# Down projection's weights and raws in the buffers of gate and up, and the last blocks' weights and features in slots that the last group does not read

## The chip, the core and the metric

One core of a Trainium2 chip runs the kernel. The metric is the device time of one execution in microseconds (us). The engines are TensorE (PE, with its weight loads as PEld), VectorE (DVE), ScalarE (ACT), GpSimd (POOL), and SyncE (SP), which issues most of the DMAs.

## What is computed

One layer of a hybrid decoder, for 1024 prompt tokens and 64 sample tokens (T = 1088 in all): a mixer (short gated convolution and a state-space scan between an input and an output projection), and behind it the feed-forward part to which the change belongs:

```python
D_MODEL = 1024
FFN_HIDDEN = -(-8 * D_MODEL // (3 * 256)) * 256      # 2816
...
    h2 = rmsnorm(x, g_ffn_pre) * (1 + scale_f) + shift_f
    f = (jax.nn.silu(h2 @ w_gate) * (h2 @ w_up)) @ w_down
    x = x + gate_f * rmsnorm(f, g_ffn_post)
```

All of it is in float32.

## The kernel before

A float32 operand is held as two parts, hi and lo, in a format that TensorE multiplies faster. `part(hi, lo, v)` makes them: ACT casts v to hi (L1039), DVE subtracts hi from v (L1040). A product is then three matmuls: hi by hi, hi by lo, lo by hi.

The hidden width 2816 is cut into 11 blocks j of 256. Gate, up and most of down use the Strassen-Winograd scheme: a `unit` makes the seven products p = 1, 5, 6, 3, 7, 2, 4 of one block of weights, in this order, each for the token halves q = 0 (PSUM banks `pm`, 256 columns) and q = 1 (banks `pz`, 288 columns). The first product into a result is copied out of PSUM by ACT (L1093), the others are added to it by DVE (L1095). ACT and DVE take their instructions in the order of the program, which a scheduler sets by its own costs; the products are held in the written order (`in_order`).

The features f = silu(gate) * up of each block are turned into hi and lo and stored to DRAM as f_d[j][q] (L1540), since they do not fit on the chip beside the weights. The last stretch of the program is:

- The last up unit, (10, [1]): block 10, half 1. Ahead of it, the raw weights of the first two down units (`raws_d`) are loaded into the pool `btp` of gate and up.
- Sixteen down units, here called u0 to u15: four groups of two blocks, g = [0,1], [2,3], [4,5], [6,7], by four pairs of row tiles mp = 0 to 3 of the output. `combos_d(g, mp)` makes a unit's seven weight combinations out of one raw tile: seven casts on ACT and seven subtractions on DVE, with four adds between them on POOL (L1652, L1654, L1655, L1658). The features of a group come back from DRAM into the slots `fc{j % 4}{q}`; those of the first group in three pieces each, the others whole, one slot at each of the units ahead (`ahead`). The results are gathered in `facc`.
- Blocks 8, 9 and 10 in plain form: `down(m)` does 18 matmuls for each of the eight row tiles m, for token tiles ts = [0,1,2,3] (block 1, 512 columns), then [4,5,6], then [7,8]. Their weights are `wd` (six tiles of 128 rows, split by `part` out of `rwd`), their features `ff`, both loaded on SP's queue: `rwd` first, then `ff` in the order of `queued_behind`, then the gate and the residual rows.
- The tail of each block (L1239 to L1256), which transposes, norms, adds the residual and stores.

Before, the down stage had pools of its own: `raw2` with five raw tiles and `wc2` with fifteen tiles of one product each. The last stage's pools were opened over them: `wdp` lay partly over `wc2`, `ff80` and `ff90` over `raw2`, and the two `rwd` buffers over slots of `fc1`. A tile in such a place waits for what used the place before.

Of the kernel before, what the change touches and what calls it, by code (L numbers as in the profile page):

```python
# [9 lines left out]
F32 = mybir.dt.float32  # L10
F32R = mybir.dt.float32r
# [5 lines left out]
P = 128  # L17
D = 1024
# [15 lines left out]
def hymba_step(ctx, tc, i, o):  # L34
    nc = tc.nc
# [992 lines left out]
    def in_turn(pools):  # L1028
        pools.append(pools.pop(0))
        return pools[-1]  # L1030
# [358 lines left out]

    left.close()  # L1390
    mid.close()
    slots = pool(left, "wcA", 4), pool(left, "wcB", 4)
    raw_from = [slots[0]] * 4
    xc0 = pool(left, "xc0", 1)
    sg0, f0, st0 = (pool(left, n, 1) for n in ("sg0", "f0", "st0"))
# [203 lines left out]
    w_from += [pool(right, "wcC", 2, side="right")] * 2  # L1599
    groups = [0, 1], [2, 3], [4, 5], [6, 7]  # L1600

    def raw_d(p, g, mp, tag="raw"):
        raw = p.tile([P, 4, 256], F32, tag=tag, name=nm("raw"))
        nc.sync.dma_start(raw, w_down[g[0] * 256:(g[-1] + 1) * 256, mp * 256:mp * 256 + 256].rearrange(
            "(k p) n -> p k n", p=P))
        return raw

    for j, qs in [(1, [1])] + [(j, [0, 1]) for j in range(2, 10)] + [(10, [0]), (10, [1])]:
        eng = nc.gpsimd if len(qs) == 2 else nc.vector
        gate_unit(j, qs, combos_w(w_gate, 256 * j, eng))  # L1610
        W = combos_w(w_up, 256 * j, eng)
        if (j, qs) == (10, [1]):

            raws_d = [raw_d(btp, groups[0], mp, "bt") for mp in range(2)]
        up_unit(j, qs, W, {}, eng)


    for stage in (left, base, right):
        stage.close()
    facc_of = [pool(right, f"facc{mp}", 1, side="right").tile([P, 2, T], F32, tag="facc", name=f"facc{mp}")  # L1620
               for mp in (3, 2, 1, 0)][::-1]
    facc = [facc_of[m // 2][:, m % 2] for m in range(KT)]
    raw2 = pool(left, "raw2", 5)
    wc2 = pool(left, "wc2", 15)
    fcp = [[pool(left, f"fc{n}{q}", 1) for q in range(2)] for n in range(4)]

    f_in, loads = {}, []
# [7 lines left out]
        f_in[j, q] = {p: [F[:, (at + s * nb + b) * n:(at + s * nb + b + 1) * n] for s in range(2)]  # L1635
                      for p, (at, nb, b) in AT.items()}

    def combos_d(g, mp):
        nk = len(g)
        raw = raws_d.pop(0) if raws_d else raw_d(raw2, g, mp)  # L1640
        A = raw.rearrange("p (k j) (i c) -> p i j k c", j=2, i=2)
        a11, a12, a21, a22 = (A[:, m, j] for m in range(2) for j in range(2))
        W = {}

        def parts_(p, b):
            t = wc2.tile([P, 2, 2, P], F32R, tag="wc2", name=nm(f"w{p}_"))[:, :, :nk]
            part(t[:, 0], t[:, 1], b)
            W[p] = [[t[:, s, k] for k in range(nk)] for s in range(2)]

        parts_(1, a11)  # L1650
        parts_(4, a22)
        nc.gpsimd.tensor_tensor(a22, a21, a22, op=add)  # L1652
        parts_(5, a22)
        nc.gpsimd.tensor_tensor(a21, a11, a21, op=sub)  # L1654
        nc.gpsimd.tensor_tensor(a11, a22, a11, op=sub)  # L1655
        parts_(6, a11)
        parts_(2, a12)
        nc.gpsimd.tensor_tensor(a12, a12, a11, op=sub)  # L1658
        parts_(3, a12)
        parts_(7, a21)  # L1660
        return W
# [7 lines left out]
    for g, nxt in itertools.zip_longest(groups, groups[1:], fillvalue=()):  # L1669
        ahead = [(j, q) for q in range(2) for j in nxt]  # L1670
        F = [{p: [[f_in[j, q][p][s] for j in g] for s in range(2)] for p in AT} for q in range(2)]
        for mp in range(4):
            W = combos_d(g, mp)

            for jq in ahead[mp:mp + 1]:
                load_f(*jq)
                nc.sync.dma_start(*loads[-1])
            out = [facc_of[mp][:, :, t0:t0 + 2 * n].rearrange("p m (h c) -> p m h c", h=2) for t0, n in QS]
            unit(W, F, len(g), [0, 1], lambda q, i, h: out[q][:, i, h], g == groups[0])


    left.close()
    ffp, rows_of = {}, []
    for at in ((8, 0), (9, 0), None, (8, 1), None, (10, 0)):
        if at:
            ffp[at] = pool(left, f"ff{at[0]}{at[1]}", 1)
        else:
            rows_of.append(pool(left, f"row{len(rows_of)}", 1))
    wdp, rwd = pool(left, "wdp", 6), pool(left, "rwd", 2)
    ffp.update({(j, 1): pool(left, f"ff{j}1", 1) for j in (9, 10)})  # L1690
    rowp, gfp, sqp = pool(left, "rowp", 11), pool(left, "gfp", 2), pool(left, "sqp", 1)

    wide = rows_of[1]
    rows_of = [rowp] * 11 + rows_of

    def row_end():
        p = in_turn(rows_of)
        return p.tile([P, 1280 if p is wide else D], F32, tag="row", name=nm("row"))[:, :D]

    def out_tail(ts):  # L1700
        res = []
# [17 lines left out]
                             ((0, 4), (4, 2), (6, 2)), (), (slice(0, 512), slice(512, D)), squares)  # L1719

    wd = []
    for k in range(6):
        v = wdp.tile([P, 2, D], F32R, tag="wd", name=nm("wd"))
        raw = rwd.tile([P, D], F32, tag="rwd", name=nm("rwd"))
        nc.sync.dma_start(raw, w_down[(16 + k) * P:(17 + k) * P, :])
        part(v[:, 0], v[:, 1], raw)
        wd.append((v[:, 0], v[:, 1]))
    ff = {}
    for q, (t0, n) in enumerate(QS):
        for j in (8, 9, 10):  # L1730
# [56 lines left out]
```

## Time and profile before

| | us |
|---|---|
| runs: lowest, median, highest of three | 1760.15, 1762.36, 1763.54 |
| profiled execution, its own time | 1754.62 |
| its span in the trace | 1752.9 |
| last up unit's end, u0's start | 1461.2 |
| u15's last add in facc | 1639.06 |
| first matmul of block 1 | 1654.96 |
| share of the span: PE, DVE, ACT, POOL | 96%, 65%, 44%, 11% |

The profiled execution is one of its own and lies 7.7 us below the median of the timed runs; sums over its rows are made against its own time. The mean granted clock of TensorE in it is 0.987 of full speed.

In rows of a timeline stand the start, the duration, the engine, the line in the kernel, the operation, out<-in, and in brackets the idle time ahead of it with what ended it; ACTq and SPq are those engines' DMA issues. In a row of windows stand, for each engine, its busy time and the number of instructions, then the granted clock of TensorE, the DMA engines' share and GB/s. A clock under 1.00 means that TensorE ran a part of that stretch at a lower speed.

### The profile page before, as it was taken

The numbers are of one execution on the slowest core, as the hardware profiler recorded it, in microseconds if no ns is written. First come the engines' busy times: TensorE is split into PE (matmuls) and PEld (weight loads), VectorE is DVE, ScalarE is ACT, GpSimd is POOL, SyncE is SP. The second block draws the span as 40 slices with busy tenths as digits, with TensorE's granted clock in tenths as the row PEclk, the third lists the DMA queues.
The fourth block names the chain that finished last, engine by engine and source line by source line (L and its number), as shares of the span: only waits on it lengthen the run. The fifth ranks groups of instructions, "written<-read, shape, count | busy, mean of one in ns | idle before, by whom it ended". The sixth has DMA issues, their size and how long they took to land.

```text
span 1752.9 us, 31332 instructions
## 1 busy us (share of the span) xinstructions
PE 1684.0 (96%) x12604; PEld 1598.2 (91%) x12604; DVE 1140.6 (65%) x2178; ACT 771.8 (44%) x1571; POOL 196.5 (11%) x293
## 2 busy tenths in 40 slices
PE   5999999999999999999999999999999999999697
PEld 4898888898999999998889999999999999999587
DVE  5588777777888686641147789566755584687434
ACT  3457454557444333322227665444544453422122
POOL 2110000000001000000000000222222002322012
PEclk9999999999999999999999999999999999999899
DMA  9210345442402421276365544334443259750433
GB/s 319 71 32 18 127 136 170 129 125 76 151 25 100 151 100 54 100 269 226 119 202 188 190 147 166 112 138 150 155 148 126 100 187 378 289 227 26 163 125 136
DMA packets 159671, 256.37 MB, mean 146 GB/s; under 512 B 10625, under 2 KB 123441, under 8 KB 157990
## 3 DMA queue, kind: packets, MB, share of 16 engines
q1 hardware_dynamic: 159238, 253.19, 41.9%
q8 instruction: 99, 1.62, 0.4%
q10 hardware_dynamic: 288, 1.18, 0.2%
q14 instruction: 46, 0.38, 0.1%
HBM read 184.63 MB, written 69.71 MB: 145 GB/s over the span
## 4 chain that ended last, share of the span: by engine, by line
PE 84%; DVE 6%; DMA 4%; ACT 3%; issue 2%; POOL 1%; SPq 1%; ACTq 0%; DVEq 0%; POOLq 0%
PE pm L334 10%; PE pm L336 10%; PE pm L335 10%; PE pz L1078 7%; PE pz L1080 7%; PE pz L1079 7%; PE pm L1078 7%; PE pm L1080 7%; PE pm L1079 7%; DMA h<-in_w_ada 1%; PE pm L209 1%; PE pz L751 1%; PE pz L745 1%; PE pz L756 1%; DMA raw<-in_w_in 1%
## 5 line engine op out<-in xcount | busy, mean ns | idle before, releaser
L312 DVE TENSOR_TENSOR wl<-raw,wh 128x512 fp32r<-128x512 f32 (+1 forms) x87 | 61.3, 729 | 99.6 <-ACT wh L311 85.8
L334 PE MATMUL pm<-h,wh 128*128 128x384 f32 (+1 forms) x342 | 114.3, 334 | 0.0
L335 PE MATMUL pm<-h,wh 128*128 128x384 f32 (+1 forms) x342 | 114.2, 334 | 0.0
L336 PE MATMUL pm<-h,wl 128*128 128x384 f32 (+1 forms) x342 | 113.5, 333 | 0.0
L336 PE MATMUL pm<-hb,wl 128*128 128x512 f32 (+2 forms) x320 | 107.3, 337 | 2.1 <-DVE wl L312 2.1
L335 PE MATMUL pm<-hb,wh 128*128 128x512 f32 (+2 forms) x320 | 107.5, 337 | 0.0
L311 ACT CAST wh<-raw 128x512 fp32r<-128x512 f32 (+1 forms) x89 | 56.4, 664 | 115.5 <-PE pm L335 72.7
L334 PE MATMUL pm<-hb,wh 128*128 128x512 f32 (+2 forms) x320 | 105.7, 337 | 1.0 <-ACT wh L311 1.0
L1040 DVE TENSOR_TENSOR fs<-f,fs 128x576 fp32r<-128x576 f32 (+2 forms) x76 | 53.5, 718 | 23.6 <-ACT fs L1039 22.8
L336 PEld LDWEIGHTS pm<-hb,wl 128*128 128x128 f32 x320 | 60.8, 190 | 7.6 <-DVE wl L312 2.4
L334 PEld LDWEIGHTS pm<-hb,wh 128*128 128x128 f32 x320 | 60.4, 190 | 6.8 <-ACT wh L311 1.2
L334 PEld LDWEIGHTS pm<-h,wh 128*128 128x128 f32 x342 | 64.8, 189 | 1.8 <-issue 0.9
L335 PEld LDWEIGHTS pm<-h,wh 128*128 128x128 f32 x342 | 64.7, 189 | 1.4 <-issue 0.7
L336 PEld LDWEIGHTS pm<-h,wl 128*128 128x128 f32 x342 | 64.7, 189 | 1.3 <-issue 1.0
L334 PE MATMUL pm<-ff,wd 128*128 128x512 f32 (+2 forms) x144 | 49.5, 344 | 16.8 <-DMA ff<-f_d 16.7
L335 PEld LDWEIGHTS pm<-hb,wh 128*128 128x128 f32 x320 | 60.7, 190 | 5.2
L1039 ACT CAST fs<-f 128x576 fp32r<-128x576 f32 (+2 forms) x76 | 44.5, 600 | 40.1 <-DMA f_d<-fs 25.0
L1095 DVE TENSOR_TENSOR facc<-facc,pz 128x288 f32<-128x288 f32 x96 | 43.3, 451 | 17.1 <-PE pz L1080 16.6
L334 PE MATMUL pm<-bt,wh 128*128 128x384 f32 (+2 forms) x146 | 50.9, 348 | 0.0
L1749 DVE TENSOR_TENSOR facc<-facc,pm 128x512 f32<-128x512 f32 (+2 forms) x24 | 12.7, 531 | 55.4 <-PE pm L336 55.4
L336 PE MATMUL pm<-ff,wd 128*128 128x512 f32 (+2 forms) x144 | 48.6, 338 | 0.0
L335 PE MATMUL pm<-ff,wd 128*128 128x512 f32 (+2 forms) x144 | 48.6, 338 | 0.0
(7118 smaller groups left out, 6331.4 us busy)
## 6 DMA issues: line engine op xcount, KB each, us to landing
raw<-in_w_in SPq DMA_DIRECT2D x48, 512.0 KB
wa<-in_w_ada SPq DMA_DIRECT2D x32, 512.0 KB
raw<-in_w_out SPq DMA_DIRECT2D x32, 512.0 KB
f_d<-fs SPq DMA_DIRECT2D x28, 576.0 KB
f_d<-fs SPq DMA_DIRECT2D x30, 512.0 KB
raw<-in_w_gate SPq DMA_DIRECT2D x28, 512.0 KB
raw<-in_w_up SPq DMA_DIRECT2D x28, 512.0 KB
y_d<-y SPq DMA_DIRECT2D x26, 544.0 KB
```

Of the source, the lines that this page charges most:

```text
L209: mm(ps[32 * j:32 * j + 32, :], cT[:, k, :], w[:, jj * 512:(jj + 1) * 512], start=(k == 0), stop=(k == KT - 1))
L311: (nc.gpsimd.tensor_copy if hi_eng else nc.scalar.copy)(wh, raw)
L312: (eng or nc.vector).tensor_tensor(wl, raw, wh, op=sub)
L334: mm(ps[:, :n], wh, xh, start=(first and j == 0), stop=False)
L335: mm(ps[:, :n], wh, xl, start=False, stop=False)
L336: mm(ps[:, :n], wl, xh, start=False, stop=(last and j == end))
L1039: nc.scalar.copy(hi, v)
L1040: (eng or nc.vector).tensor_tensor(lo, v, hi, op=sub)
L1078: mm(ps, W[0][k], X[0][k], start=(start and k == 0), stop=False, skip_group_check=True)
L1079: mm(ps, W[0][k], X[1][k], start=False, stop=False, skip_group_check=True)
L1080: mm(ps, W[1][k], X[0][k], start=False, stop=(stop and k == nk - 1), skip_group_check=True)
L1095: nc.vector.tensor_tensor(out(q, i, h), out(q, i, h), ps, op=add)
```

## The change

It has three parts.

1. The down units' raws go into `btp` (four tiles), and their weight combinations into `wcA` and `wcB` of gate and up, two products to one tile in the order of their use: 1 and 5, 6 and 3, 7 and 2, 4. A unit takes four of the eight tiles. `raw2` and `wc2` go, and `btp`, `wcA` and `wcB` are closed at the end of the down units only.
2. The four adds of `combos_d` are on DVE for group [0,1], and on POOL as before for the others.
3. The last stage is laid out anew. `wdp` and `ff90` lie over the slots of blocks 4 and 5, which the group [6,7] does not read. `ff80` and `ff100` lie over `btp`, and the halves 1 of the features over `wcA`, `wcB` and feature slots. The raw buffer of `wd` is the place of `ff90`: three loads of 256 rows use it one after the other instead of six of 128 rows through two buffers. There are 13 row tiles as before.

```diff
     left.close()
     mid.close()
-    slots = pool(left, "wcA", 4), pool(left, "wcB", 4)
+    kept_pools = ExitStack()
+    slots = pool(kept_pools, "wcA", 4), pool(kept_pools, "wcB", 4)
...
-    def raw_d(p, g, mp, tag="raw"):
-        raw = p.tile([P, 4, 256], F32, tag=tag, name=nm("raw"))
+    def raw_d(g, mp):
+        raw = btp.tile([P, 4, 256], F32, tag="bt", name=nm("raw"))
...
-    for stage in (left, base, right):
-        stage.close()
+    left.close()
+    right.close()
...
-    raw2 = pool(left, "raw2", 5)
-    wc2 = pool(left, "wc2", 15)
     fcp = [[pool(left, f"fc{n}{q}", 1) for q in range(2)] for n in range(4)]
...
-    def combos_d(g, mp):
+    w_from = [slots[0]] * 4 + [slots[1]] * 4
+
+    def combos_d(g, mp, eng):
         nk = len(g)
-        raw = raws_d.pop(0) if raws_d else raw_d(raw2, g, mp)
+        raw = raws_d.pop(0) if raws_d else raw_d(g, mp)
...
+        pair = [in_turn(w_from).tile([P, 2, 2, 2, P], F32R, tag="wc", name=nm("wd")) for _ in range(4)]
+
         def parts_(p, b):
-            t = wc2.tile([P, 2, 2, P], F32R, tag="wc2", name=nm(f"w{p}_"))[:, :, :nk]
+            n = (1, 5, 6, 3, 7, 2, 4).index(p)
+            t = pair[n // 2][:, n % 2]
             part(t[:, 0], t[:, 1], b)
...
-        nc.gpsimd.tensor_tensor(a22, a21, a22, op=add)
+        eng.tensor_tensor(a22, a21, a22, op=add)
         parts_(5, a22)
-        nc.gpsimd.tensor_tensor(a21, a11, a21, op=sub)
-        nc.gpsimd.tensor_tensor(a11, a22, a11, op=sub)
+        eng.tensor_tensor(a21, a11, a21, op=sub)
+        eng.tensor_tensor(a11, a22, a11, op=sub)
...
-        nc.gpsimd.tensor_tensor(a12, a12, a11, op=sub)
+        eng.tensor_tensor(a12, a12, a11, op=sub)
...
-            W = combos_d(g, mp)
+            W = combos_d(g, mp, nc.vector if g == groups[0] else nc.gpsimd)
...
-    left.close()
-    ffp, rows_of = {}, []
-    for at in ((8, 0), (9, 0), None, (8, 1), None, (10, 0)):
...
-    wdp, rwd = pool(left, "wdp", 6), pool(left, "rwd", 2)
-    ffp.update({(j, 1): pool(left, f"ff{j}1", 1) for j in (9, 10)})
-    rowp, gfp, sqp = pool(left, "rowp", 11), pool(left, "gfp", 2), pool(left, "sqp", 1)
+    for stage in (left, kept_pools, base):
+        stage.close()
...
+    ff_pools((8, 0), (10, 0), (8, 1))
+    rowa = pool(left, "rowa", 2)
+    ff_pools((9, 1))
+    rowb = pool(left, "rowb", 2)
+    wdp = pool(left, "wdp", 6)
+    ff_pools((9, 0), (10, 1))
+    rowp, gfp, sqp = pool(left, "rowp", 9), pool(left, "gfp", 2), pool(left, "sqp", 1)
+    rows_of = [rowa] * 2 + [rowb] * 2 + [rowp] * 9
...
-    for k in range(6):
-        v = wdp.tile([P, 2, D], F32R, tag="wd", name=nm("wd"))
-        raw = rwd.tile([P, D], F32, tag="rwd", name=nm("rwd"))
-        nc.sync.dma_start(raw, w_down[(16 + k) * P:(17 + k) * P, :])
-        part(v[:, 0], v[:, 1], raw)
-        wd.append((v[:, 0], v[:, 1]))
+    for k in range(0, 6, 2):
+        raw = ffp[9, 0].tile([P, 2, D], F32, tag="ff", name=nm("rwd"))
+        nc.sync.dma_start(raw, w_down[(16 + k) * P:(18 + k) * P, :].rearrange("(k p) n -> p k n", p=P))
+        for kk in range(2):
+            v = wdp.tile([P, 2, D], F32R, tag="wd", name=nm("wd"))
+            part(v[:, 0], v[:, 1], raw[:, kk])
+            wd.append((v[:, 0], v[:, 1]))
```

The order of the instructions moves at three places. In the names of both kernels raw_1668 and raw_1669 are the raws of u0 and u1; w1 to w7 are combinations, w3__1666 and w7__1667 those of the last up unit. In the names of after, a combination's tile is wd_ as well (wd_1680 to wd_1683 for u0, wd_1691 to wd_1694 for u1), and wd_1867 to wd_1874 are the six tiles of blocks 8 to 10.

On DVE, from the last up unit to u0. Before:

```order
L1095 TENSOR_TENSOR f_1670_15643<-f_1670_15643,pz_1672_15658 128x288
L1095 TENSOR_TENSOR f_1670_15643<-f_1670_15643,pz_1671_15644 128x288
L1095 TENSOR_TENSOR f_1670_15643<-f_1670_15643,pz_1673_15711 128x288
L1040 TENSOR_TENSOR w1__1680_15822<-raw_1668_15639,w1__1680_15822 128x256
L1040 TENSOR_TENSOR w4__1681_15825<-raw_1668_15639,w4__1681_15825 128x256
L1040 TENSOR_TENSOR w5__1682_15829<-raw_1668_15639,w5__1682_15829 128x256
L1525 TENSOR_TENSOR f_1670_15643<-f_1670_15643,sg_1655_15514 128x1152
```

After, the same stretch begins inside the last up unit's own combinations:

```order
L1040 TENSOR_TENSOR w3__1666_15633<-raw_1660_15612,w3__1666_15633 128x512
L1657 TENSOR_TENSOR raw_1668_15639<-raw_1668_15639 128x2x128
L1659 TENSOR_TENSOR raw_1668_15639<-raw_1668_15639 128x2x128
L1040 TENSOR_TENSOR wd_1680_15813<-raw_1668_15639,wd_1680_15813 128x256
L1660 TENSOR_TENSOR raw_1668_15639<-raw_1668_15639 128x2x128
L1040 TENSOR_TENSOR w7__1667_15636<-raw_1659_15610,w7__1667_15636 128x512
L1040 TENSOR_TENSOR wd_1681_15814<-raw_1668_15639,wd_1681_15814 128x256
L1040 TENSOR_TENSOR wd_1682_15815<-raw_1668_15639,wd_1682_15815 128x256 x2
L1663 TENSOR_TENSOR raw_1668_15639<-raw_1668_15639 128x2x128
L1040 TENSOR_TENSOR wd_1681_15814<-raw_1668_15639,wd_1681_15814 128x256
L1040 TENSOR_TENSOR wd_1691_15941<-raw_1669_15641,wd_1691_15941 128x256
L1095 TENSOR_TENSOR f_1670_15643<-f_1670_15643,pz_1672_15658 128x288
```

All of u0's combinations, with their four adds, now stand on DVE ahead of the last three adds into f; before, they stood behind them.

On ACT, at the last two units. Before, the casts into wd follow all the casts of u15:

```order
L1039 CAST w2__1905_17824<-raw_1900_17807 128x256
L1039 CAST w3__1906_17828<-raw_1900_17807 128x256
L1039 CAST w7__1907_17831<-raw_1900_17807 128x256
L1039 CAST wd_1914_17987<-rwd_1915_17988 128x1024
L1039 CAST wd_1916_17992<-rwd_1917_17993 128x1024
L1039 CAST wd_1918_17997<-rwd_1919_17998 128x1024
```

After (raw_1844 and raw_1855 are the raws of u14 and u15):

```order
L1039 CAST wd_1846_17628<-raw_1844_17625 128x256
L1039 CAST wd_1870_17938<-rwd_1869_17936 128x1024
L1039 CAST wd_1871_17941<-rwd_1869_17936 128x1024
L1039 CAST wd_1859_17758<-raw_1855_17753 128x256
L1039 CAST wd_1856_17755<-raw_1855_17753 128x256
L1039 CAST wd_1857_17756<-raw_1855_17753 128x256
L1039 CAST wd_1858_17757<-raw_1855_17753 128x256 x2
L1039 CAST wd_1857_17756<-raw_1855_17753 128x256
L1039 CAST wd_1873_17946<-rwd_1872_17944 128x1024
L1039 CAST wd_1874_17949<-rwd_1872_17944 128x1024
```

The casts of the second load now stand ahead of u15's; those of the first (wd_1867, wd_1868) stand further up among u14's, and those of the third behind u15's.

On SP, the loads behind the last raws. Before:

```order
L1604 DMA raw_1900_17807<-in_w_down 128x4x256
L1725 DMA rwd_1915_17988<-in_w_down 128x1024
L1725 DMA rwd_1917_17993<-in_w_down 128x1024
L1725 DMA rwd_1919_17998<-in_w_down 128x1024
L1725 DMA rwd_1921_18003<-in_w_down 128x1024
L1725 DMA rwd_1923_18008<-in_w_down 128x1024
L1725 DMA rwd_1925_18013<-in_w_down 128x1024
L1445 DMA ff_1926_18017<-f_d8_0_140 128x1024 x2
```

After:

```order
L1605 DMA raw_1855_17753<-in_w_down 128x4x256
L1732 DMA rwd_1866_17928<-in_w_down 128x2x1024
L1732 DMA rwd_1869_17936<-in_w_down 128x2x1024
L1732 DMA rwd_1872_17944<-in_w_down 128x2x1024
L1446 DMA ff_1875_17952<-f_d8_0_140 128x1024 x2
L1446 DMA ff_1876_17955<-f_d9_0_142 128x1024 x2
L1446 DMA ff_1877_17958<-f_d10_0_144 128x1024 x2
```

Three loads of 1 MB stand where six of 0.5 MB stood, ahead of the same feature loads.

More of the change, by code (lines that the diff above doesn't have):

```diff
@@ L1612, in hymba_step @@
         if (j, qs) == (10, [1]):
-            raws_d = [raw_d(btp, groups[0], mp, "bt") for mp in range(2)]
+            raws_d = [raw_d(groups[0], mp) for mp in range(2)]
         up_unit(j, qs, W, {}, eng)
-    for stage in (left, base, right):
-        stage.close()
+    left.close()
+    right.close()
     facc_of = [pool(right, f"facc{mp}", 1, side="right").tile([P, 2, T], F32, tag="facc", name=f"facc{mp}")
@@ L1679, in hymba_step, with ff_pools @@
             unit(W, F, len(g), [0, 1], lambda q, i, h: out[q][:, i, h], g == groups[0])
-    left.close()
-    ffp, rows_of = {}, []
-    for at in ((8, 0), (9, 0), None, (8, 1), None, (10, 0)):
[L1685 to L1688, printed above, removed]
-    wdp, rwd = pool(left, "wdp", 6), pool(left, "rwd", 2)
-    ffp.update({(j, 1): pool(left, f"ff{j}1", 1) for j in (9, 10)})
-    rowp, gfp, sqp = pool(left, "rowp", 11), pool(left, "gfp", 2), pool(left, "sqp", 1)
-    wide = rows_of[1]
-    rows_of = [rowp] * 11 + rows_of
+    for stage in (left, kept_pools, base):
+        stage.close()
+    ffp = {}
+    def ff_pools(*at):
+        for j, q in at:
+            ffp[j, q] = pool(left, f"ff{j}{q}", 1)
+    ff_pools((8, 0), (10, 0), (8, 1))
[6 more added lines that the diff above has]
+    rows_of = [rowa] * 2 + [rowb] * 2 + [rowp] * 9
     def row_end():
-        p = in_turn(rows_of)
-        return p.tile([P, 1280 if p is wide else D], F32, tag="row", name=nm("row"))[:, :D]
+        return in_turn(rows_of).tile([P, D], F32, tag="row", name=nm("row"))
     def out_tail(ts):
```

## The prediction

> **What bounds the kernel now.** First the page of the profile: its span, TensorE's share, and TensorE (PE) and its granted clock over 40 slices of 43.8 us.
>
> ```profile
> span 1752.9 us, 31332 instructions
> PE 1684.0 (96%) x12604; PEld 1598.2 (91%) x12604; DVE 1140.6 (65%) x2178; ACT 771.8 (44%) x1571; POOL 196.5 (11%) x293
> PE   5999999999999999999999999999999999999697
> PEclk9999999999999999999999999999999999999899
> ```
>
> TensorE is the bound, so only its gaps and its slow clock can be won. Between the first and the last slice only the 38th is weak (1621 to 1665 us): the last down units and the first block behind them. TensorE's waits for the lines of the down projection (line, releaser: us, times, longest):
>
> ```profile
> PE pm L334 <- DMA ff<-f_d: 16.7, 3, 15.9
> PE pm L1078 <- ACT facc L1093: 3.2, 2, 2.8
> PE pm L1078 <- DVE facc L1095: 1.8, 2, 1.4
> ```
>
> Then windows cut at the unit starts: the last up unit, u0 to u5, u13, u15, the gap, the rest of the first row of block 1 (one of its eight row tiles m), and the seven rows after it.
>
> ```profile
> core 0: us, PE busy (x) PEld busy (x) DVE busy (x) ACT busy (x) POOL busy (x), PEclk, DMA share, GB/s
> 1450.70:1461.20 10.50, 10.50 (x82) 10.50 (x81) 2.73 (x6) 3.33 (x7) 0.13 (x1) 1.00 1.02 414
> 1461.20:1476.90 15.70, 12.75 (x87) 12.02 (x85) 10.16 (x19) 6.86 (x19) 6.04 (x8) 0.89 0.88 342
> 1476.90:1487.43 10.53, 10.53 (x86) 10.53 (x85) 4.50 (x11) 4.42 (x13) 2.68 (x4) 1.00 1.05 417
> 1487.43:1498.87 11.44, 11.07 (x87) 10.60 (x85) 5.57 (x14) 5.96 (x19) 3.76 (x6) 1.00 0.93 333
> 1498.87:1510.13 11.26, 10.85 (x86) 10.60 (x85) 6.46 (x18) 6.26 (x19) 4.18 (x6) 1.00 0.29 91
> 1510.13:1523.00 12.87, 11.30 (x87) 10.66 (x85) 9.18 (x25) 4.45 (x13) 4.86 (x7) 1.00 1.00 400
> 1523.00:1533.48 10.48, 10.48 (x86) 10.48 (x85) 8.88 (x23) 2.85 (x7) 3.01 (x4) 1.00 0.92 359
> 1607.00:1617.48 10.48, 10.48 (x86) 10.48 (x85) 8.38 (x22) 2.85 (x7) 3.08 (x5) 1.00 0.01 2
> 1628.60:1639.10 10.50, 10.43 (x84) 10.19 (x82) 6.09 (x15) 0.04 (x1) 0.00 (x0) 1.00 0.01 2
> 1639.10:1654.90 15.80, 0.00 (x0) 0.00 (x0) 7.22 (x7) 6.13 (x6) 0.00 (x0) 0.62 0.59 186
> 1654.90:1663.10 8.20, 7.29 (x19) 4.53 (x20) 0.46 (x1) 0.00 (x0) 0.00 (x0) 0.68 1.02 403
> 1663.10:1691.70 28.60, 28.60 (x128) 23.63 (x127) 4.82 (x8) 0.00 (x0) 0.00 (x0) 1.00 0.53 190
> ```
>
> An undisturbed unit is 10.48 us (u5, u13). Over that, u0 loses 5.22, u1 0.05, u2 0.96, u3 0.78, u4 2.39: 9.40 us at the transition. At the other end TensorE stands still for 15.8 us and then runs at clock 0.68. The timelines of that place:
>
> ```profile
> 1639.06 1.99 ACT L1039 CAST wd<-rwd 128x1024 fp32r<-128x1024 f32 x2 [22.16 <-PE pz L1080]
> 1654.13 1.23 DVE L1040 TENSOR_TENSOR wd<-rwd,wd 128x1024 fp32r<-128x1024 f32 x1 [1.51 <-ACT wd L1039]
> 1596.92 52.60 SPq L1725 DMA_DIRECT2D rwd<-in_w_down  x6
> 1649.63 10.15 SPq L1445 DMA_DIRECT2D ff<-f_d  x12
> 1639.06 0.46 DVE L1095 TENSOR_TENSOR facc<-facc,pz 128x288 f32<-128x288 f32 x1 [0.37 <-PE pz L1080]
> 1663.11 0.69 DVE L1749 TENSOR_TENSOR facc<-facc,pm 128x512 f32<-128x512 f32 x1 [7.75 <-PE pm L336]
> ```
>
> The first cast into wd waits for the last product (1639.06). Its raw buffers come free one by one, so SP is held in its six rwd loads for 52.6 us, and the ff loads behind them start only at 1649.63. The wait is booked to ff, but it begins with where wd lies.
>
> **The change, part by part.** *Term A, the last group into block 1.* The order shows the wd casts and subtractions between the combinations of u13 to u15, and the ff loads behind three rwd loads. Block 1's first row can then end one period after the last unit: a row is 28.60/7 = 4.09 us (last window); the last unit's last add stands at 1639.06, the add of row 0 at 1663.11, and 24.05 - 4.09 = 19.96 us go. That includes the slow clock: matmuls start 0.42 apart in the first 5 us, some eleven of them, later 0.23.
>
> ```profile
> 1655.53 0.63 PE L335 MATMUL pm<-ff,wd 128*128 128x512 f32 x1
> 1655.95 0.63 PE L336 MATMUL pm<-ff,wd 128*128 128x512 f32 x1
> 1663.14 0.39 PE L335 MATMUL pm<-ff,wd 128*128 128x512 f32 x1
> 1663.37 0.39 PE L336 MATMUL pm<-ff,wd 128*128 128x512 f32 x1
> ```
>
> Does everything land in time? In before, the first rwd load goes at u12's start (1596.92), when u11 has left its slot; so it will now. Throughput over 1595 to 1665 us, in slices of 1.75 us:
>
> ```profile
> GB/s 0 105 363 131 9 0 0 0 0 0 0 0 9 0 0 0 0 0 0 0 0 0 9 0 0 0 0 295 225 80 236 192 318 250 344 414 421 418 413 411
> ```
>
> 1 MB goes through slices 2 to 4, so it has landed 4.6 us after its issue, as estimated from this row. One buffer serves three loads, and a load waits for both splits of the one before. A load and its two splits (1.04 and 1.23 each, the casts ahead of the subtractions) are some 8.1 us bare; between the unit's own rows I put them at one unit, 10.5: the third is split at u14 + 10.4 us. Then ff90, by the same row, lands at u14 + 15.0, and ff100, 1 MB at 411 GB/s or 2.5 us on, at u14 + 17.5; u15 ends at u14 + 20.96. Slack 3.5 us. ff80 goes into raw buffers that are free earlier. The loads of the other half and the gate and residual rows then start earlier than before, with block 1 (8 × 4.09 = 32.7 us) as cover; without it each 1 MB would cost 2.5 us.
>
> *Term B, the transition.* Before, u0's combinations go from DVE to POOL to ACT to DVE in turn, and start only when the last up unit drains.
>
> ```profile
> 1469.48 0.58 PE L1078 MATMUL pm<-fc,w__1685_15841 128*128 128x256 f32 x1 [2.84 <-ACT facc L1093]
> 1466.84 0.41 ACT L1039 CAST w__1685_15841<-raw 128x256 fp32r<-128x256 f32 x1 [0.85 <-POOL raw L1658]
> 1466.90 1.81 ACTq L1540 DMA_DIRECT2D f_d<-fs  x2
> 1465.53 1.28 POOL L1658 TENSOR_TENSOR raw<-raw 128x256 f32<-128x256 f32 x1 [2.03 <-DVE w__1684_15837 L1040]
> 1460.18 0.42 DVE L1040 TENSOR_TENSOR w__1680_15822<-raw,w__1680_15822 128x256 fp32r<-128x256 f32 x1
> 1462.28 0.63 DVE L1040 TENSOR_TENSOR w__1682_15829<-raw,w__1682_15829 128x256 fp32r<-128x256 f32 x1 [1.34 <-ACT w__1682_15829 L1039]
> ```
>
> ACT's copies out of PSUM, which release the bank, queue behind a cast that waits for POOL, and behind two stores. In the order of after, u0's and u1's combinations stand among those of the last up unit, 7 to 10 us earlier, and group 0's adds are on DVE. An add of that shape costs DVE about the 0.42 of the subtraction, 1.7 a unit, where u1 to u3 leave it 4.8 to 6 us free (windows). What stays: in u0 the third feature pieces and the two stores on ACT (1.81 us), estimated 1.0 us; in u3 and u4, where group 1 uses POOL as before and DVE is at 9.18 of 12.87, 0.9. So 9.4 - 1.9 = 7.5 us go. Bounds: 0 (the copies stay late for the stores' sake) and 9.4. I take 7.5, since only 1.81 of the chain stays on ACT. Two units' 14 subtractions and 8 adds are 9.2 us of DVE, into a stretch that has 7.8 free and, for u1's part, u0 behind it. Six of them stand ahead of the last up unit's w3 and w7 (2.5 us); if PE waits for these I allow 1 us, in the upper end alone.
>
> *Term C, the wd splits move beside units.* DVE gets six subtractions, ACT six casts:
>
> ```profile
> L1039 ACT CAST wd<-rwd x6: 1039/1044/1045, 1639.1 to 1653.1; 128x1024 fp32r<-128x1024 f32 x6
> L1040 DVE TENSOR_TENSOR wd<-rwd,wd x6: 1218/1226/1226, 1640.1 to 1654.1; 128x1024 fp32r<-128x1024 f32 x6
> ```
>
> ACT (2.85 of 10.48 busy) hides 2.1 a unit. DVE has 10.48 - 8.38 = 2.1 free in u13 and gets 2 × 1.23 = 2.45: a lag of 0.35 a unit, 1.05 after three, which u15 with 4.4 us free works off. A bank is used again one product pair (10.48/7 = 1.50 us) after it is full, and the add that reads it takes 0.46: PE bears 1.04 us of lag, but a single 1.23 ahead of an add can exceed it. I take +0.5. Bounds: 0, and 6 × 1.23 - 3 × 1.6 (u5's free time) = 2.6, plus 1.3 if each subtraction meets a POOL add and stretches as the 0.63 above does against 0.42: +3.9.
>
> The longest of POOL's four adds, 0.80 us in the mean (group by form):
>
> ```profile
> L1655 POOL TENSOR_TENSOR raw<-raw 128x256 f32<-128x256 f32 x16 | 12.8, 800 | 1.3
> ```
>
> Here a rule speaks against the change: the Trainium skill, "SBUF — State Buffer", section "SBUF: two separate sides", has a VectorE operation with two SBUF inputs and a GpSimd operation exclude each other for the whole instruction. The 0.63 row next to a POOL add agrees in kind. By the rule six subtractions could each lose a POOL add's 0.80, 4.8 us of DVE (estimate), and the sum would be a gain of 22 or 23 instead of 27. I keep the row's 0.21 each, in the upper bound alone, since POOL is busy 3.08 of 10.48 in u13.
>
> The rest (smaller pool count, 293 to 277 POOL rows, closing of pools) costs TensorE nothing: POOL is 11% busy. The pairing of two products in one tile frees weights up to 1.5 us later; u5 and u13 show PE without a wait, with the combinations of a unit needed a unit later.
>
> **Sum.** -20.0 - 7.5 + 0.5 = -27.0 us: the profiled execution 1754.6 becomes 1727.6. That execution lies 7.7 us below the median of the three runs, 1762.36; I predict the median, 1735.4.
>
> **Rivals.** R1: only block 1 gains; u0 to u4 lose their 9.4 again, because the copies wait behind stores and the features' loads (342 and 417 GB/s in u0 and u1, near the most any window shows). -19.5: 1742.9. For it: DMA share 0.88 to 1.05 there. Against: the bank wait of 2.84 names ACT, not a load.
>
> R2: the chain of one raw buffer takes 13 us a load, not 10.5. Then ff100 lands 7.5 - 3.5 = 4.0 us after u15: 1739.4, and 1741.6 if the clock drops as well (eleven matmuls × 0.2 = 2.2). For it: the third load's casts stand behind all of u15's. Against: 13 us is 4.9 over the bare 8.1, half a unit of queueing at each load. The Trainium skill, "TensorE: Matmul & The Clock Gate", section "What's actually happening", halves the clock after about 3.4 us idle; the 15.8 us gap with 0.42 spacing after it agrees, and by it R2 stands just at the edge.
>
> R3, slower: eight tiles of two products instead of fifteen of one make units wait for weights. A tile is free only when both its products are done, and ACT's casts for unit n+2 stand in a queue; if that makes each unit late by more than 27/16 = 1.7 us, all is lost; at 2 us a unit, +5: 1767. Against: u5 and u13 make a whole unit's combinations within 8.9 us of DVE, and tiles of unit n are free before n+1 ends.
>
> R4: the wd splits still wait for u15 by some overlap, and only B counts: 1754.9.
>
> **How the numbers follow.** Main case 0.64 (1731.5 to 1739), R1 0.16, R2 0.10, R4 0.03, R3 0.05, faster than the main case 0.02. A change under 0.2% (3.5 us) can't be told from none here. Faster: 0.64 + 0.16 + 0.10 + 0.03 + 0.02 = 0.95; R3 is slower for 0.04 and near its break-even for 0.01, the same. The range reaches from B's 9.4 with C at nothing, 1733.0, less 4 for the runs' own spread (1760.15 to 1763.54), 1729, to R1 with most of C's bound, 1746. R3 and R4 and the far ends of the others lie outside.
>
> **What would show it.** Right: no wait at L334 on ff above 1 us, clock 1.00 up to block 1; u0 below 12 us; wd subtractions before the last unit's end; units u12 to u15 at 10.5. A: wrong, if ff's wait at L334 stays over 3 us. B: wrong, if u0 to u4 sum to over 58 us (52.4 + 5.6). C: wrong, if u12 to u15 sum to over 43.5. The forecast fails as a whole if units u5 to u11 grow beyond 10.6.

## The result and the profile after

The changed kernel takes 1733.13 us in the median of its runs (1729.44 to 1734.12), the kernel before 1762.17 (1760.15 to 1763.54): a ratio of 0.9832, 95% interval 0.9815 to 0.985, or 29 us less. The prediction said 1735.4, with a range of 1729 to 1746. The profiled execution of the changed kernel took 1732.75 us, 21.9 less than the profiled one of before; why the two differences differ is taken up in the first experiment.

The page of the profile after: span, engines, and TensorE with its granted clock over 40 slices.

```profile
span 1731.0 us, 31270 instructions
PE 1682.0 (97%) x12604; PEld 1600.0 (92%) x12604; DVE 1147.9 (66%) x2194; ACT 770.9 (45%) x1571; POOL 185.7 (11%) x277
PE   5999999999999999999999999999999999999997
PEclk9999999999999999999999999999999999999999
```

The weak slice near the end is gone, and TensorE's busy time is nearly the same: what went is idle time and slow clock. Of TensorE's waits for lines of the down projection, the 16.7 us for ff and the 3.2 for ACT's copies are no longer in the list; the longest that is left (line and releaser: us in all, times, longest) is:

```profile
PE pm L1078 <- DVE facc L1095: 1.4, 2, 1.0
```

Windows of the changed kernel, cut as before: u0, u2, u4, u13, u14, u15, the first row of block 1.

```profile
core 0: us, PE busy (x) PEld busy (x) DVE busy (x) ACT busy (x) POOL busy (x), PEclk, DMA share, GB/s
1465.52:1476.25 10.73, 10.73 (x87) 10.58 (x85) 6.15 (x12) 4.26 (x11) 0.00 (x0) 1.00 0.99 404
...
1486.78:1498.01 11.23, 10.92 (x87) 10.63 (x85) 8.50 (x24) 5.66 (x17) 0.00 (x0) 1.00 1.01 391
...
1508.58:1521.01 12.43, 11.00 (x86) 10.59 (x85) 8.48 (x23) 3.92 (x11) 4.88 (x7) 1.00 1.01 418
...
1605.28:1615.81 10.53, 10.53 (x86) 10.53 (x85) 9.86 (x23) 4.75 (x10) 4.00 (x6) 1.00 0.30 101
1615.81:1626.46 10.65, 10.65 (x86) 10.60 (x85) 10.54 (x23) 3.44 (x6) 2.73 (x4) 1.00 0.59 197
1626.46:1636.99 10.53, 10.53 (x86) 10.53 (x85) 6.50 (x16) 0.00 (x0) 0.00 (x0) 1.00 0.83 313
1636.99:1641.30 4.31, 4.31 (x21) 3.57 (x20) 0.46 (x1) 0.00 (x0) 0.00 (x0) 1.00 0.70 244
```

u0 is down from 15.70 to 10.73 us, u4 from 12.87 only to 12.43, and the first row of block 1 starts with u15's end, at full clock. The timeline of that end:

```profile
1594.94 21.90 SPq L1732 DMA_DIRECT2D rwd<-in_w_down  x3
1621.35 17.86 SPq L1446 DMA_DIRECT2D ff<-f_d  x12
1600.96 1.23 DVE L1040 TENSOR_TENSOR wd<-rwd,wd 128x1024 fp32r<-128x1024 f32 x1 [0.36 <-ACT wd L1039]
1624.67 1.22 DVE L1040 TENSOR_TENSOR wd<-rwd,wd 128x1024 fp32r<-128x1024 f32 x1
1637.19 0.46 DVE L1095 TENSOR_TENSOR facc<-facc,pz 128x288 f32<-128x288 f32 x1 [0.38 <-PE pz L1080]
1641.30 0.69 DVE L1758 TENSOR_TENSOR facc<-facc,pm 128x512 f32<-128x512 f32 x1 [3.65 <-PE pm L336]
```

The splits run from 1600.96 to 1625.89, eleven us before u15 ends, and the features are issued from 1621.35 on. From the last unit's last add to the add of row 0 it is 4.11 us, where it was 24.05.

All kernels, by their profiles (each window is worked out from the starts of the units and of the two adds in the timeline), with the median of the runs, and the ratio to the runs of the kernel before on the same chip:

| kernel | median us | ratio, 95% interval | u0 | u0 to u4 | u5 to u11 | u12 to u14 | last add to row 0's add | u0's start to row 0's add |
|---|---|---|---|---|---|---|---|---|
| before | 1762.17 | 1 | 15.70 | 61.80 | 73.73 | 31.60 | 24.05 | 201.91 |
| changed | 1733.13 | 0.9832 (0.9815 to 0.985) | 10.73 | 55.49 | 73.74 | 31.71 | 4.11 | 175.78 |
| again (the same) | 1730.73 | 0.9846 (0.9828 to 0.9865) | 10.54 | 54.88 | 73.73 | 31.71 | 4.10 | 175.16 |
| start_only | 1750.12 | 0.9959 (0.9945 to 0.9973) | 10.54 | 54.62 | 73.74 | 31.60 | 22.57 | 193.26 |
| end_only | 1738.84 | 0.9889 (0.9876 to 0.9903) | 17.19 | 63.31 | 73.74 | 31.60 | 4.11 | 183.49 |
| pool_adds | 1732.33 | 0.9854 (0.9839 to 0.9868) | 11.53 | 56.51 | 73.73 | 31.71 | 4.10 | 176.79 |
| own_pools_dve | 1756.34 | 0.9987 (0.9971 to 1.0003) | 13.23 | 57.94 | 73.73 | 31.60 | 24.54 | 198.54 |
| late_wd | 1755.86 | 0.9987 (0.9972 to 1.0002) | 11.81 | 56.72 | 73.73 | 31.60 | 29.14 | 201.92 |
| six_loads | 1731.81 | 0.9863 (0.9829 to 0.9898) | 10.54 | 55.33 | 73.73 | 32.34 | 4.11 | 177.13 |
| dve_all | 1731.93 | 0.9852 (0.9822 to 0.9882) | 10.54 | 52.90 | 73.73 | 31.60 | 6.00 | 174.96 |
| early_raws | 1729.45 | 0.9843 (0.9818 to 0.9868) | 10.84 | 52.97 | 73.73 | 31.71 | 4.11 | 173.25 |

The last columns begin at u0. What a kernel loses ahead of it they do not hold; pool_adds loses 1.95 us there, as is shown below. The median of before was 1758.15 on the chip of again, start_only, end_only and pool_adds, 1758.96 on that of late_wd, six_loads, dve_all and early_raws, and 1757.32 on that of own_pools_dve.

### The profile page after: what moved, and what is told of

Its sections match the earlier page's. It is cut to its first block, busy times and chain, and to the rows that moved or that the text cites. A ratio compares the mean times of both kernels' runs of the same rounds, so it can differ in the third digit from the quotient of the medians.

```text
span 1731.0 us, 31270 instructions
## 1 busy us (share of the span) xinstructions
PE 1682.0 (97%) x12604; PEld 1600.0 (92%) x12604; DVE 1147.9 (66%) x2194; ACT 770.9 (45%) x1571; POOL 185.7 (11%) x277
## 5 line engine op out<-in xcount | busy, mean ns | idle before, releaser
L1039 ACT CAST wd<-raw 128x256 fp32r<-128x256 f32 x112 | 42.9, 406 | 96.1 <-PE pz L1080 33.6
L1078 PE MATMUL pz<-fc,wd 128*128 128x288 f32 x224 | 66.2, 295 | 0.0
L1080 PE MATMUL pz<-fc,wd 128*128 128x288 f32 x224 | 66.0, 295 | 0.0
L1079 PE MATMUL pz<-fc,wd 128*128 128x288 f32 x224 | 65.9, 294 | 0.0
L1078 PE MATMUL pm<-fc,wd 128*128 128x256 f32 x224 | 63.3, 283 | 1.4 <-DVE facc L1095 1.4
L1040 DVE TENSOR_TENSOR wd<-raw,wd 128x256 fp32r<-128x256 f32 x112 | 54.4, 494 | 14.6 <-ACT wd L1039 14.2
L1080 PE MATMUL pm<-fc,wd 128*128 128x256 f32 x224 | 63.1, 282 | 0.3 <-DVE wd L1040 0.3
```

Source lines behind the costliest of these rows:

```text
L1039: nc.scalar.copy(hi, v)
L1040: (eng or nc.vector).tensor_tensor(lo, v, hi, op=sub)
L1078: mm(ps, W[0][k], X[0][k], start=(start and k == 0), stop=False, skip_group_check=True)
L1079: mm(ps, W[0][k], X[1][k], start=False, stop=False, skip_group_check=True)
L1080: mm(ps, W[1][k], X[0][k], start=False, stop=(stop and k == nk - 1), skip_group_check=True)
```

## The experiments

### The same kernel once more (again)

No edit.

> The changed kernel once more, for the interval and for the part that did not change. Theory: the change is worth 26 us in its own stretch (u0's start to the add of block 1's first row: 26.1 us shorter in the two profiles), and the 29 us between the medians hold about 3 us of run-to-run differences; then the two profiles differ ahead of u0 by something between -4 and +4 us that is not the change's, and the ratio lies near 0.985. Rival: the change also saves 3 us outside that stretch; then the ratio comes out at 0.983 again and the part ahead of u0 or behind the first add is shorter too.

The ratio is 0.9846, 27.4 us on this chip, and the stretch from u0's start to row 0's add is 26.8 us shorter than before (201.91 to 175.16); in the first pair of profiles 26.1. Ahead of u0 the three kernels issue the same matmuls, yet u0 starts at 1461.2 us in the profile of before, at 1465.5 in the changed one, at 1467.9 here; behind row 0's add the three differ by 0.1 us (89.8, 89.7, 89.7). So the change is worth 26 to 27 us in its own stretch. The first theory holds but for a size: ahead of u0 the two profiles of the changed kernel are 4.3 and 6.7 us later than that of before, where up to 4 was allowed. That is why the first pair of profiles shows only 21.9; that the 29 of the medians have the same source is likely and not shown, since one execution of each kernel was profiled. The records of the granted clock in the traces have TensorE at half rate ahead of u0 for 17.0 us in the profile of before, 27.2 in the changed kernel's and 30.6 in this one. A busy TensorE loses half of what is added, 5.1 and 6.8 us, and u0 starts 4.3 and 6.7 us later. One such stretch is seen in the window of 452 to 460 us, first of before, then of the changed kernel:

```profile
452.00:460.00 8.00, 8.00 (x66) 7.47 (x62) 4.51 (x19) 0.47 (x1) 0.00 (x0) 1.00 0.21 66
```

```profile
452.00:460.00 8.00, 8.00 (x59) 7.64 (x59) 3.44 (x17) 0.47 (x1) 0.00 (x0) 0.79 0.22 68
```

TensorE counts as busy through both, at clock 1.00 in the one and 0.79 in the other, seven matmuls fewer in 8 us.

### The two ends apart (start_only, end_only)

start_only is the changed kernel with the last stage of before; end_only is the kernel before with the new last stage:

```diff
 # start_only, against the changed kernel
     for stage in (left, kept_pools, base):
         stage.close()
-    ff_pools((8, 0), (10, 0), (8, 1))
...
+    for at in ((8, 0), (9, 0), None, (8, 1), None, (10, 0)):
...
+    wdp, rwd = pool(left, "wdp", 6), pool(left, "rwd", 2)
...
-    for k in range(0, 6, 2):
+    for k in range(6):
 # end_only, against the kernel before
-    for at in ((8, 0), (9, 0), None, (8, 1), None, (10, 0)):
...
-    wdp, rwd = pool(left, "wdp", 6), pool(left, "rwd", 2)
...
+    ff_pools((8, 0), (10, 0), (8, 1))
...
-    for k in range(6):
+    for k in range(0, 6, 2):
```

> The change's parts 1 and 2 alone (weights and raws in the kept buffers, adds of group 0 on VectorE), with the last stage laid out and loaded as before. Theory, the two ends are independent: u0 to u4 take 55.5 us as in the changed kernel, the wait at block 1's first row is 16 us as before, gain 6 us, about 1756. Rival: the shorter transition is eaten by the later wait, because the loads of the last stage and not the units set when block 1 begins; then the gap before block 1 grows by 6 us and the time is that of before, 1762.

> The change's part 3 alone: the last stage's layout and the three loads, with the own raw and weight pools and the adds on GpSimd as before. Theory: the last stage's gain of 20 us comes from the layout alone; no wait at block 1, u0 to u4 61.8 us as before, about 1742. Rival: the layout needs the early raws and weight tiles too (its splits come too late when the weights have pools of their own); then a wait of several us stays at block 1's first row and the gain is under 16 us.

start_only gains 8.0 us in the medians (1758.15 to 1750.12; 6 were expected), end_only 19.3 (to 1738.84); together 27.3, and the whole change on this chip 27.4. The ends are independent, and both first theories hold. In start_only the gap before block 1 is there as before, though by the sizes of the pools only the first wd tile lies over weights that u15 reads (the end of wcB):

```profile
1634.55:1649.81 15.26, 0.15 (x3) 0.03 (x1) 6.94 (x7) 4.86 (x5) 0.00 (x0) 0.61 0.60 198
```

In end_only it is gone, while u0 keeps its late weights and slow clock:

```profile
1463.54:1480.73 17.19, 14.23 (x87) 13.49 (x86) 10.53 (x19) 7.27 (x21) 6.35 (x8) 0.80 0.92 365
...
1642.72:1647.03 4.31, 4.31 (x21) 3.57 (x20) 0.46 (x2) 0.00 (x0) 0.00 (x0) 1.00 0.88 304
```

### Which part of the start (pool_adds, own_pools_dve)

pool_adds puts the adds of group 0 back on POOL; own_pools_dve is the kernel before with these adds on DVE:

```diff
 # pool_adds, against the changed kernel
-            W = combos_d(g, mp, nc.vector if g == groups[0] else nc.gpsimd)
+            W = combos_d(g, mp, nc.gpsimd)
 # own_pools_dve, against the kernel before
+        eng = nc.vector if g == groups[0] else nc.gpsimd
...
-        nc.gpsimd.tensor_tensor(a22, a21, a22, op=add)
+        eng.tensor_tensor(a22, a21, a22, op=add)
```

> The changed kernel with group 0's four adds on GpSimd, as before. Theory: it is the early start of u0's and u1's combinations, not the engine of the adds, that shortens u0; u0 stays under 12 us, u0 to u4 lose 1 to 3 us more than the changed kernel's 55.5, time +1 to +3 over the changed kernel. Rival: the four hand-overs between VectorE, GpSimd and ScalarE are what made u0 15.7 us; then u0 goes back to about 15 us and 4 to 5 us are lost.

> The kernel before with one thing changed: group 0's four adds on VectorE. It is the fourth corner beside own pools with GpSimd's adds (u0 15.7 to 17.2 us), kept buffers with GpSimd's adds (11.5) and kept buffers with VectorE's (10.5). Theory: the late start of u0's combinations, which the own pools cause, is the larger part; with VectorE's adds alone u0 still takes 12.5 to 14.5 us and 1 to 3 us are gained in u0 to u4. Rival: with own pools the hand-overs to GpSimd are the larger part, so VectorE's adds alone bring u0 under 11.5 us and 5 us in all; then the two parts of the change overlap, and each alone would have been enough.

u0's window in pool_adds, then in own_pools_dve:

```profile
1461.71:1473.24 11.53, 11.08 (x87) 10.61 (x85) 6.09 (x12) 4.14 (x11) 0.78 (x1) 1.00 0.87 331
```

```profile
1466.14:1479.37 13.23, 11.56 (x87) 10.75 (x85) 11.42 (x27) 7.33 (x20) 0.00 (x0) 1.00 0.86 338
```

With the changed kernel these are the four corners. u0 to u4 take 61.8 us with own pools and POOL's adds, 57.9 with own pools and DVE's, 56.5 with kept buffers and POOL's, 54.9 to 55.5 with both. But pool_adds pays a second time, ahead of u0: from the first matmul of the last up unit to u0's start it takes 13.10 us, where before, own_pools_dve and the changed kernel take 11.15. There TensorE waits for a copy into f, which stands on ACT behind a cast for u0, and that cast for POOL:

```profile
1448.61:1461.71 13.10, 11.69 (x86) 11.22 (x85) 7.09 (x15) 6.74 (x17) 4.96 (x7) 1.00 1.02 414
```

```profile
1450.70 0.41 ACT L1039 CAST wd<-raw 128x256 fp32r<-128x256 f32 x1 [1.61 <-POOL raw L1660]
1452.89 0.39 ACT L1093 COPY f<-pz 128x288 f32<-128x288 f32 x1
1453.33 0.40 PE L1078 MATMUL pz<-x__1243_10982,w__1664_15626 128*128 128x288 f32 x1 [1.38 <-ACT f L1093]
```

From the last up unit's start to u4's end the kept buffers alone thus bring 3.3 us (72.95 to 69.61), the adds alone 3.9 (to 69.09), both 6.3 to 6.9 (to 66.64 and 66.04). The two gains add up, as far as single profiles can tell: start_only, six_loads and late_wd start as the changed kernel does, and their u0 to u4 take 54.62, 55.33 and 56.72 us, so that a profile is good to some 2 us. Which part is the larger is not shown by the profiles. In the medians the kept buffers, with POOL's adds, are worth 6.5 us on top of end_only (1738.84 to 1732.33, with intervals that lie apart), while own_pools_dve is not told apart from the kernel before (1.0 us lower, the interval reaches 1.0003), nor pool_adds from the changed kernel. So the medians bear out the theory that the early start is the larger part. The adds alone brought more in their profile than its 1 to 3 us; u0's 13.23 lies in its range.

### Only the place of wd (late_wd)

```diff
-    ff_pools((8, 0), (10, 0), (8, 1))
+    ff_pools((8, 0), (10, 0))
+    wdp = pool(left, "wdp", 6)
+    ff_pools((8, 1))
     rowa = pool(left, "rowa", 2)
     ff_pools((9, 1))
     rowb = pool(left, "rowb", 2)
-    wdp = pool(left, "wdp", 6)
     ff_pools((9, 0), (10, 1))
```

> The changed kernel with wdp moved down in the last stage, over the weight tiles of the last two units; ff80, ff90, ff100, the raw buffer and the three loads stay where they are. Theory: the place of wd alone decides. The splits wait for u14's and u15's weights again, the third load and ff90 wait for the splits: u15 + 12.5 us for the second load's splits, + 4.6 load, + 2.4 splits, + 7.1 for ff90 and ff100 = u15 + 26.6 against u15's end at + 10.5: a wait of 14 to 16 us at block 1 and 2 us of slow clock, about 17 us slower than the changed kernel. Rival: the early features (ff80, ff90, ff100 in places that are free before the end) are what gained the 20 us; then the wait is 8 us or less, the time of the splits alone.

ff81, ff91 and four row tiles move into the room that wd leaves; row 0 reads none of them. Everything that the end had gained is lost again and 5 us more (29.14 us between the two adds, 24.05 before); the median is not told apart from that of before (the interval reaches 1.0002). The wait, the first casts, SP's queue and the window of the gap:

```profile
PE pm L334 <- DMA ff<-f_d: 20.8, 2, 17.7
```

```profile
1627.13 2.00 ACT L1039 CAST wd<-rwd 128x1024 fp32r<-128x1024 f32 x2 [8.34 <-PE pz L1080]
1638.03 2.35 DVE L1040 TENSOR_TENSOR wd<-rwd,wd 128x1024 fp32r<-128x1024 f32 x2
1595.52 53.62 SPq L1733 DMA_DIRECT2D rwd<-in_w_down  x3
1649.24 13.54 SPq L1446 DMA_DIRECT2D ff<-f_d  x12
```

```profile
1637.46:1655.30 17.84, 0.16 (x2) 0.01 (x1) 5.59 (x6) 3.57 (x4) 0.00 (x0) 0.56 0.46 167
```

The place of wd decides: the early features and the three loads gain nothing while the raws ahead of them on SP wait. That wd's place would be enough without them was not tried. The loss against the changed kernel is 25 us, not 17: row 0 itself takes 11.5 us, with a second wait for ff of 3.1, and the first wait is 17.8 us, not 14 to 16: the first casts could run at u14's end (1627.13), but their subtractions came at 1638.03, behind u15's last add, since DVE works in the order of its queue. SP stands 53.6 us in three loads, as it stood 52.6 in six.

### The chain through one raw buffer (six_loads)

```diff
-    for k in range(0, 6, 2):
-        raw = ffp[9, 0].tile([P, 2, D], F32, tag="ff", name=nm("rwd"))
+    for k in range(6):
+        raw = ffp[9, 0].tile([P, D], F32, tag="ff", name=nm("rwd"))
```

> The changed kernel with six loads of 128 rows through the one raw buffer instead of three of 256. In the changed kernel the splits end at u14 + 9.9 us, where 10.4 was estimated, and some 4 us are left until u15 ends. Theory: the chain of load, cast, subtraction, next load sets when ff90 can start, and six smaller links need 6 to 7.5 us each, 36 to 45 us from u12's start, where the three took 31: the slack of 4 us is used up, and block 1 waits 1 to 10 us. Rival: the places in the queues of ScalarE and VectorE set the chain, not the loads; then the splits end at the same time as before and nothing is lost.

A link takes 6.1 us (subtractions from 1595.48 to 1625.80, five links), the low end of the theory, and the splits end 36.4 us after u12's start. Block 1 does not wait, so the theory has the chain right and its wait wrong: the splits end 3.75 us nearer to u15's end than in the changed kernel, so that the rival falls too. The price came elsewhere: u14 takes 11.28 us and u15 11.43, where 10.65 and 10.53 stood.

```profile
PE pm L1078 <- DVE facc L1095: 2.0, 3, 1.0
PE pz L1078 <- DVE facc L1095: 0.6, 1, 0.6
```

```profile
1624.72 1.05 ACT L1039 CAST wd<-rwd 128x1024 fp32r<-128x1024 f32 x1 [5.12 <-DMA rwd<-in_w_down]
1625.80 1.23 DVE L1040 TENSOR_TENSOR wd<-rwd,wd 128x1024 fp32r<-128x1024 f32 x1 [1.52 <-ACT wd L1039]
```

DVE stands idle in front of a split whose load is late (1.52 us at the last one), and the adds that free a PSUM bank stand behind it. That is 1.5 us in two units; the waits in the list explain 1.2 of it (2.0 and 0.6, less the 1.4 that the changed kernel has too). The median is not told apart from the changed kernel's.

### VectorE filled up (dve_all)

```diff
-            W = combos_d(g, mp, nc.vector if g == groups[0] else nc.gpsimd)
+            W = combos_d(g, mp, nc.vector)
```

> The changed kernel with the four adds of all sixteen units on VectorE. Theory (the sum of VectorE's work by unit decides): u5 to u11 stay at 10.53 us, since 8.4 and 4 x 0.42 make 10.1 of 10.5; u12 to u14, with 2.45 us of splits each on top, are 2 us over and lose 3 to 5 us together; u4 loses its wait for the adds on GpSimd (1.9 us) to a part. Together 1 to 4 us slower than the changed kernel. Rival: adds and splits wait in VectorE's queue where nothing is late; all units 10.53, u4 too, and 2 us are gained.

The theory of VectorE's sum by unit falls. All units from u3 to u15 take 10.53 or 10.54 us, u4 too. The windows of u4, u13 (the one with the most work on DVE) and u15:

```profile
1510.85:1521.39 10.54, 10.54 (x87) 10.54 (x86) 9.71 (x28) 3.55 (x10) 0.00 (x0) 1.00 1.04 425
...
1605.65:1616.19 10.54, 10.54 (x87) 10.54 (x86) 10.36 (x30) 4.85 (x10) 0.00 (x0) 1.00 0.28 102
...
1626.72:1637.25 10.53, 10.53 (x86) 10.53 (x85) 7.97 (x16) 2.01 (x2) 0.00 (x0) 1.00 0.59 220
```

The excess goes into the combinations, which are made up to a unit ahead, and is paid from u15's free time (7.97 us of DVE there, 6.50 in the changed kernel); the adds that PE needs stay in place. What it costs is the splits' end:

```profile
1633.31 1.22 DVE L1040 TENSOR_TENSOR wd<-rwd,wd 128x1024 fp32r<-128x1024 f32 x1
```

```profile
PE pm L334 <- DMA ff<-f_d: 1.1, 3, 0.4
```

The last split ends at 1634.53, 2.7 us before u15, and row 0 is 1.9 us late. The splits could thus end 8 us later than in the changed kernel (1625.89, 11.1 us before u15's end) for a price of 2 us. What u4 gains is thus lost at row 0: the whole stretch is 0.2 to 0.8 us shorter than the changed kernel's, and the median is not told apart.

### A version from the readings (early_raws)

```diff
     for piece in range(3):
         for to, src in loads[piece::3]:
             nc.sync.dma_start(to, src)
+    raws_d += [raw_d(groups[0], mp) for mp in (2, 3)]
...
-            W = combos_d(g, mp, nc.vector if g == groups[0] else nc.gpsimd)
+            W = combos_d(g, mp, nc.vector if g in groups[:2] else nc.gpsimd)
```

The reading behind it, in the changed kernel: SP issues two feature loads of group 1 over 12.86 us, and u2's raw goes behind them.

```profile
1464.41 12.86 SPq L1682 DMA_DIRECT2D fc<-f_d  x2
1477.33 0.69 SPq L1605 DMA_DIRECT2D raw<-in_w_down  x1
```

> A version made from the readings: the raws of u2 and u3 are loaded ahead of the features of group 1 (in the changed kernel SyncE stands 13 us in the first of these feature loads, and u2's raw lands at its heels), and the adds of groups 0 and 1 are on VectorE. Theory: u2 loses its 0.3 to 0.7 us, u4 its 1.9, all units 10.53 but 0.2; 2 us faster than the changed kernel. Rival: u4 is late for the landing of its raws and not for the adds on GpSimd; then u4 still takes 12 us and nothing measurable is gained.

u2 and u4 now take a unit's time:

```profile
1485.41:1495.94 10.53, 10.53 (x86) 10.53 (x85) 4.15 (x10) 3.93 (x11) 0.00 (x0) 1.00 0.99 400
1506.48:1517.01 10.53, 10.53 (x86) 10.53 (x85) 9.71 (x28) 3.54 (x10) 0.00 (x0) 1.00 1.03 406
```

dve_all, with the loads as they were, leaves u2 at 10.75 and brings u4 to 10.54; so u4's 1.9 us are the adds on POOL. That u2's loss is the raw behind the features is not shown: with the loads as they were, u2 takes 11.23 us in the changed kernel, 10.79 in again and 10.53 in start_only. From u0's start to row 0's add it is 173.25 us, 1.9 to 2.5 less than the changed kernel. In the medians (ratio 0.9843 against 0.9846 and 0.9832) this can't be told: it is in the profile, and not shown as a time.

## Why the prediction was right

**Term A** was -19.96 and is -19.94 (24.05 to 4.11). Its steps hold one by one. The wait booked to ff began with wd's place: late_wd. The first rwd load goes at u12's start + 0.2 us. The third split was put at u14 + 10.4 and ended at 1625.89, u14 + 10.1. The slack of 3.5 us was put too short: dve_all's splits end 8.4 us later against u15's end and cost 1.9, so by these two it is some 6.5. R2 (a chain of 13 us a load) did not come (10.9 and 9.9 us from one load's last subtraction to the next one's), and six_loads shows that even twice the links keep block 1 on time here, at 1.5 us in the units.

**Term B** was -7.5 and is -6.3 in the first profile, -6.9 in the second. Its base was 0.25 us too large: the windows of u5 and u13 end 0.05 us before the next unit starts, a unit takes 10.53 us, and u0 to u4 lost 9.15 over that, not 9.40. The sum was nearly right, its parts were not: u0 was left 1.0 us and keeps 0.2 at most, u2 was left nothing and keeps 0.3 to 0.7, u4 was left under 0.9 and keeps 1.9. The term that was mis-sized is u4: the hand-overs to POOL of group 1 were seen, but priced at less than they had cost before. u4's third product (p = 6) waits for an add on DVE that stands behind a subtraction, which waits for ACT, and that for POOL:

```profile
1510.54 0.41 ACT L1039 CAST wd<-raw 128x256 fp32r<-128x256 f32 x1 [1.29 <-POOL raw L1660]
1510.98 0.42 DVE L1040 TENSOR_TENSOR wd<-raw,wd 128x256 fp32r<-128x256 f32 x1 [1.07 <-ACT wd L1039]
1512.20 0.41 DVE L1095 TENSOR_TENSOR facc<-facc,pm 128x256 f32<-128x256 f32 x1
1512.76 0.36 PE L1078 MATMUL pm<-fc,wd 128*128 128x256 f32 x1 [1.02 <-DVE facc L1095]
```

R1 (the start keeps its loss, for the loads' sake) is refuted by u0's 10.73 us at a DMA share of 0.99. The 1 us that the upper end allowed for the last up unit did not come either: 11.15 us before and after.

**Term C** was +0.5 and is +0.1, u14's 10.65. DVE came out as full as was worked out (9.86 and 10.54 us busy in u13 and u14), but a full DVE does not make PE late while the work that slips is the next unit's combinations. The lag of 1.04 us that PE was said to bear applies only to what stands ahead of an add in the queue; dve_all, with the four adds of every unit on DVE too, shows no loss in the units (at most 10.36 us of DVE, in u13), six_loads, with a split that waits, does.

**R3** (eight tiles of two products make units late) did not come: u5 to u11 take 73.73 us before and 73.74 after, to the hundredth.

The rule of the Trainium skill, "SBUF — State Buffer", section "SBUF: two separate sides", that a VectorE operation with two SBUF inputs and a GpSimd operation exclude each other for the whole instruction, is borne out in kind by the one split that meets a POOL add in u13:

```profile
1614.76 1.64 DVE L1040 TENSOR_TENSOR wd<-rwd,wd 128x1024 fp32r<-128x1024 f32 x1
1614.58 0.74 POOL L1657 TENSOR_TENSOR raw<-raw 128x256 f32<-128x256 f32 x1 [4.59 <-DVE wd L1040]
1615.40 1.61 POOL L1659 TENSOR_TENSOR raw<-raw 128x256 f32<-128x256 f32 x1
```

The split begins while POOL's first add runs and takes 0.42 us more than its 1.22; POOL's second add begins while the split runs and takes 1.61 where the first took 0.74. One strictly behind the other, the three would fill 2.70 us (0.74, 1.22 and 0.74); they fill 2.43, so by these spans the exclusion is not whole here. The prediction's 0.21 for such a meeting was half of the 0.42 measured. In dve_all, without POOL's adds, no split is over 1.23. The prediction's rule-based sum, 4 us less gain, did not come because one split of six met an add, not all six, and because DVE's lag is not PE's.

The median came 2.3 us below the forecast, while the stretch itself gained 0.9 us less than the sum of 27.0. The forecast carried the gain over to the median of before; that the runs' remaining difference lies ahead of u0 is shown for the profiles ("again") and not for the runs. That the sum came within 1 us is in part luck: u4 and u2 keep some 1.0 and 0.3 to 0.7 us more than was put, u0 0.8 or more less, and C came 0.4 lower.

## What to carry to other kernels

When a wait is booked to a transfer, go back along its queue: here SP stood in loads of raws whose buffers waited for splits, whose target lay over tiles of the last unit, and putting that one target back (late_wd) cost 25 us. Weigh work added to a busy engine by what stands behind it in the queue and how far ahead that is made, not by the sum of a stage: a full VectorE cost 0.1 us, a VectorE waiting for loads 1.5. When parts of a change are tried alone, look ahead of the stretch that was cut out as well: pool_adds' loss of 1.95 us stood one unit ahead of u0, and without it the two cures of the start would seem to overlap (5.3 and 3.9 us alone, 6.3 to 6.9 together).

## What the hardware showed beside

Executions of the same matmuls differ by more than was expected ahead of the change: over the eleven profiles u0 starts between 1461.20 us (before) and 1468.49 (dve_all). In the changed kernel's profile matmuls of one shape start 0.32 us apart up to 457.3 us, and 0.17 apart behind it:

```profile
456.97 0.52 PE L335 MATMUL pm<-h,wh 128*128 128x384 f32 x1
457.29 0.50 PE L336 MATMUL pm<-h,wl 128*128 128x384 f32 x1
...
458.15 0.34 PE L334 MATMUL pm<-h,wh 128*128 128x384 f32 x1
458.32 0.34 PE L335 MATMUL pm<-h,wh 128*128 128x384 f32 x1
```

The slow stretch begins at 453.9 us, behind short transposes, and lasts 3.4 us; in the profile of before the same matmuls run at full clock. The Trainium skill, "TensorE: Matmul & The Clock Gate", section "What's actually happening", gives the activity window as 3.4 us and free-running, so that the same kernel loses a different number of matmuls in each run; these rows agree with it in length, and that the window's phase is the cause is not shown. A single profile per kernel tells a change of some us only within its own stretch, and of a part of it, as u0 to u4, only to some 2 us.
